# A hybrid decoder layer in float32: first products by arrival, one triangle product fewer, values' products turned round, bias rows in fp32r

## The chip, the cores and the metric

The kernel runs on one core of a Trainium2 chip. The metric is the device time of one execution in microseconds; before the change it is 813.0 us, the median of three runs (812.77 to 813.18). TensorE multiplies (PE in the profile; its weight loads are PEld), VectorE is DVE, ScalarE is ACT, GpSimd is POOL, and SyncE (SP) issues most of the loads.

## The reference

One decoder layer on 512 rows of 1024 columns. A normalized input is projected once; three token mixers read the projection: attention in a sliding window of 128 with sinks and a T5 bias by distance, stick-breaking attention, and attention to 256 rows of memory. Each mixer's output is gated, the three are summed and projected, and a SwiGLU network follows. What the change touches is the stick-breaking mixer and the bias:

```python
z = einsum('bqhd,bkhd->bhqk', q, k) * (d ** -0.5)
log_1m = where(causal, log_sigmoid(-z), 0.0)
between = lax.cumsum(log_1m, axis=3, reverse=True) - log_1m
a = where(causal, exp(log_sigmoid(z) + between), 0.0)
out = einsum('bhqk,bkhd->bqhd', a, v)
```

It has 8 heads of width 64 and 4 blocks of 128 rows. The bias of the window is `rel_bias[t5_bucket(dist)]`, one row of distances per head.

## The kernel before

**Number formats.** Most products keep float32 accuracy with three products of the type fp32r: an operand is split into a high part (a ScalarE copy, line 134) and the rest (a VectorE subtraction, line 135), and `mm3` (lines 166 to 168) adds high by high, high by low, low by high. `mm` (line 171) is one product in the type of its operands. A product of plain float32 operands shows as two instructions, called passes here.

**Streams.** Dense work (projections `kb`, `qb`, `ka`, `qa`, gates `g`, values `pv`, memory keys `pmk` and values `pmv`, branch outputs) lies in one list of units. `Stream` loads weights ahead, splits them ahead and gives the products out in small pieces. The attention code calls `dn.run(us)` between its steps, so that some microseconds of dense products stand between one step and the next in the program.

**Order.** The instructions go through the framework's scheduler, which keeps program order as priority and lets later work go ahead of work whose operands it holds to be late. The start alone is ordered by hand (lines 503 to 545). PSUM has a pool of two banks for dense work (`dps`) and one of six (`aps`) for attention.

**Start.** Eleven products on zeros (`WARM`) come first. Then the first three weight matrices (`his`, `los`), which arrive in pieces, meet the eight chunks of x (`u[k]`, high `uh`, low `ul`, lines 237 and 238). Three generators, one for each matrix, are advanced in turn; each turn is one `mm3`. So chunk 0 is multiplied as three products for matrix 0, three for matrix 1, three for matrix 2, and so on.

**Bias rows.** `band_bias` (lines 567 to 595) copies the table on GpSimd, multiplies it by a one-hot matrix in one float32 product of 384 columns over 32 rows, adds the window's mask on VectorE and stores the rows through DRAM. It follows the values' projection, whose results VectorE takes out of PSUM into `v_all` (line 333).

**A head of stick-breaking attention** (`sb_head`, lines 605 to 673). Scores lie with keys on partitions: key block j needs only the queries from block j on, so the four blocks have 512, 384, 256 and 128 columns. Blocks 0 and 1 fill the tiles `z[0]` and `z[1]`; blocks 2 and 3 share `z[2]`. ScalarE and VectorE make the softplus `e` and its parts `sh` and `sl`; of `e[2]` a further 128 columns hold the sum of blocks 2 and 3. Then the running sums over keys are added in PSUM: a triangle of -1 (`ntri_r`) within each block, a matrix of -1 (`none_r`) for the later blocks. Blocks 0 to 2 use the two fp32r parts, block 3 uses plain float32 (`ntri`, lines 660 and 661). Three exponentials (line 663, in the order of the tiles) give the weights, and 3 us of dense work follow. After the odd head of a pair, eight products with `v_all` add up the pair's output `ysb` in one bank: four key blocks for the even head on partitions 0 to 63 and four for the odd head on partitions 64 to 127, block 0 (512 columns) first, the even head ahead of the odd one (lines 670 to 672). In plain float32 these are 16 passes for each of four pairs.

Of the kernel before, what the change touches and what calls it, by code (L numbers as in the profile page):

```python
# [10 lines left out]
F32 = mybir.dt.float32  # L11
# [3 lines left out]
ALU = mybir.AluOpType  # L15
# [11 lines left out]
SWA, SB, MEM = 0, 1, 2  # L27
LOAD_AHEAD = 4
SPLIT_AHEAD = 3
WARM = 11  # L30


class Stream:
# [70 lines left out]
def tile_kernel(ctx, tc, a):  # L104
# [22 lines left out]
    def aps(name):  # L127
        return psa.tile([P, 512], F32, tag="a", name=name)
# [39 lines left out]
        nc.tensor.matmul(out, ll, rh, start=False, stop=stop, skip_group_check=True)  # L168

    def mm(out, l, r, start, stop):  # L170
        nc.tensor.matmul(out, l, r, start=start, stop=stop, skip_group_check=True)  # L171

    def cols(hl, o, n):
        return hl[0][:, o : o + n], hl[1][:, o : o + n]
# [86 lines left out]
    def stack_twice(kind, idx, t):  # L261

        for e in range(2):
# [9 lines left out]
            nc.vector.tensor_copy(x[o : o + 64, :], t[r : r + 64, :])  # L273
            st[(kind + "s", idx, e)] = x

    def proj(kind, idx):
        def gen(hi, lo):
            ps = (aps if kind == "kb" or (kind, idx) == ("qb", 2) else dps)(f"{kind}{idx}")
            for k in range(KC):
                mm3(ps[:, :], cols((hi, lo), k * P, P), u[k], k == 0, k == KC - 1)  # L280
                yield 0.65
            t = ck(f"{kind}{idx}")
            s = 0.125 if kind in ("qa", "qb") else 1.0

            def evac():
                with tc.high_priority():
                    nc.vector.scalar_tensor_tensor(t[:, :], ps[:, :], s, st["rb"][:, :], op0=ALU.mult, op1=ALU.mult)  # L287
                if kind in ("kb", "qa"):
                    stack_parts(kind, idx, t)
                elif kind in ("qb", "ka"):  # L290
                    stack_twice(kind, idx, t)
                elif kind == "qm":
                    st[("qms", idx)] = parts(f"qms{idx}", t)

            if "rb" in st:
                evac()
            else:
                st.setdefault("waiting", []).append(evac)
            st[(kind, idx)] = t

        return gen
# [43 lines left out]
    def vcols(t, lo):  # L345
        return v_all[:, t * 640 + lo : t * 640 + lo + 64]
# [156 lines left out]
    with tc.manual_schedule():  # L503

        idle = cst.tile([P, 512], BF16, name="idle")
        nc.vector.memset(idle[:, :], 0.0)
        pw = dps("warm")
        for i in range(WARM):
            mm(pw[:, :], idle[:, :P], idle[:, :], True, True)

        first_load(nc.scalar, 0)
        first_table = nc.scalar.preload_act_table_set("natural_log_exp_and_others")
        load_x(0, 3)
        first_load(nc.sync, 1)
        load_x(3, 5)
        first_load(nc.sync, 2)
        load_x(5, 8)
        dn.loaded = dn.have = FIRST
        first_split(0, 0)
        gain_split(0)  # L520
        for i in range(1, FIRST):
            first_split(i, 0)
        gain_split(1)
        gain_split(2)
        for p in (1, 2):
            for i in range(FIRST):
                first_split(i, p)
            for k in range(*PIECE[p]):
                if u[k] is None:
                    gain_split(k)  # L530
        xacc = ck("xacc")
        nc.scalar.activation(xacc[:, :], xraw[0][:, :], AF.Square)
        for k in range(1, KC):
            nc.scalar.activation(xraw[k][:, :], xraw[k][:, :], AF.Square)
            nc.vector.tensor_tensor(xacc[:, :], xacc[:, :], xraw[k][:, :], op=ALU.add)
        dn.ahead(4, 3)
        gens = [dn.units[i]["mm"](his[i], los[i]) for i in range(FIRST)]
        for k in range(KC + 1):
            for g in gens:
                next(g, None)  # L540
        dn.at = FIRST
        st["rs"], st["rb"] = rstd_of("x", xacc, S, aps)
        st["chain"] = since[-1]
        for f in st.pop("waiting"):
            f()
# [21 lines left out]
    def band_bias():  # L567
        oh = ck("oh")
        nc.sync.dma_start(oh[:32, :384], a["onehot"])
        rbt = ck("rbt")  # L570
        nc.sync.dma_start(rbt[:32, :8], a["rel_bias"])
        wm = ck("wm")
        nc.sync.dma_start(wm[:, :384], a["winmask"])

        rb16 = ck("rb16")
        nc.gpsimd.tensor_copy(
            rb16[:32, :P].rearrange("b (h j) -> b h j", h=8), rbt[:32, :8].unsqueeze(2).to_broadcast([32, 8, 16])
        )
        ps = aps("pbias")
        mm(ps[:, :384], rb16[:32, :P], oh[:32, :384], True, True)  # L580
        row = ck("brow")
        nc.vector.tensor_tensor(row[:, :384], ps[:, :384], wm[:, :384], op=ALU.add)
        scr = drm.tile([8, P * 384], F32, name="bscr")
        nc.gpsimd.dma_start(
            scr[:, :].rearrange("h (j m i) -> (h j) m i", j=16, m=8),
            row[:, :384].unsqueeze(1).to_broadcast([P, 8, 384]),
        )
        out = []
        for i in range(4):
            b = ck(f"bias{i}")  # L590
            src = scr[2 * i : 2 * i + 2, 127:383]
            src = bass.AP(src.tensor, src.offset, [[383, P], [P * 384, 2], [1, 256]])
            nc.gpsimd.dma_start(b[:, :].rearrange("p (h k) -> p h k", h=2), src)
            out.append(b)
        return out
# [9 lines left out]
    def sb_head(h):  # L605
        c = h // 2
        ks, qs, ql = (st[(x, c, h % 2)] for x in ("kbs", "qbs", "qbl"))
        z = [aps(f"z{h}{i}") for i in range(3)]

        def seg(ts, j):  # L610
            i, o, n = SEG[j]
            return ts[i][:, o : o + n]

        for j in range(4):
            i, o, n = SEG[j]
            kj = slice(j * P, (j + 1) * P)
            if j < 3:
                out, qh, qlo = z[i][:, o : o + n], qs[:, j * P :], ql[:, j * P :]
            else:

                out = z[i][:, o : o + 2 * n]
                qh = qs[:, j * P :].unsqueeze(1).to_broadcast([P, 2, P])
                qlo = ql[:, j * P :].unsqueeze(1).to_broadcast([P, 2, P])
            mm(out, ks[:, kj], qh, j < 3, False)
            mm(out, ks[:, kj], qlo, False, False)

        for i in range(2):
            mm(z[i][:, :P], identb[:, :], negm[:, :], False, False)
        blocks23 = z[2][:, :].rearrange("p (b n) -> p b n", b=4)[:, 0:4:2, :]
        mm(blocks23, identb[:, :], negm[:, :].unsqueeze(1).to_broadcast([P, 2, P]), False, False)  # L630
        e = [ck(f"e{h}{i}") for i in range(3)]
        sh = [ck(f"sh{h}{i}", F32R) for i in range(3)]
        sl = [ck(f"sl{h}{i}", F32R) for i in range(3)]
        for i in range(3):
            x, n = e[i][:, : W[i]], W[i]
            nc.scalar.activation(x, z[i][:, :n], AF.Abs)
            fn(x, x, AF.Exp, scale=-1.0)
            st["chain"] = fn(x, x, AF.Ln, bias=1.0)
            nc.vector.scalar_tensor_tensor(x, z[i][:, :n], 0.0, x, op0=ALU.max, op1=ALU.add)  # L639
            if i == 2:  # L640

                nc.vector.tensor_tensor(e[i][:, 384:], e[i][:, 128:256], e[i][:, 256:384], op=ALU.add)
                x, n = e[i][:, :], 512
            nc.vector.tensor_copy(sh[i][:, :n], x)
            nc.vector.tensor_tensor(sl[i][:, :n], x, sh[i][:, :n].bitcast(F32), op=ALU.subtract)
        yield 7.0

        def both(t):

            return t[2][:, :].rearrange("p (b n) -> p b n", b=4)[:, 0:4:3, :]  # L650

        for j in range(3):
            for t in (sh, sl):
                mm(seg(z, j), ntri_r[:, :], seg(t, j), False, j == 2 and t is sl)
        for t in (sh, sl):
            mm(z[0][:, 128:], none_r[:, :], seg(t, 1), False, False)
        for t in (sh, sl):
            mm(z[0][:, 256:], none_r[:, :], both(t), False, t is sl)
            mm(z[1][:, 128:384], none_r[:, :], both(t), False, t is sl)
        mm(z[2][:, 128:256], none[:, :], seg(e, 3), False, True)  # L660
        mm(seg(z, 3), ntri[:, :], seg(e, 3), False, True)
        for i in range(3):
            fn(e[i][:, : W[i]], z[i][:, : W[i]], AF.Exp)
        yield 3.0
        if h % 2 == 0:
            st["even"] = e
            return

        ys = aps(f"ysb{c}")
        for j in range(4):  # L670
            for i, x in enumerate((st["even"], e)):
                mm(ys[64 * i : 64 * i + 64, j * P :], vcols(j, 128 + (2 * c + i) * 64), seg(x, j), j == 0, j == 3)
        pair_out(SB, c, ys)


# [728 lines left out]
```

## Time and profile before

| | us |
|---|---|
| median of three runs | 813.0 |
| the profiled execution | 813.07 |
| its span | 811.3 |
| PE busy in it | 802.9 |
| DVE busy | 588.7 |
| ACT busy | 439.6 |

The 1.8 us between the profiled execution's time and its span lie outside the program's instructions. In the timeline a row gives the start, the length, the engine, the line and the operation; equal instructions that follow one another are one row with their count, under the shape of the first. The length of a product goes on into the next one's, so the cost of a product in a dense row of them is the distance between two starts. In brackets stand the idle time of the engine before the row and what ended it.

### The profile page before, as it was taken

The numbers are of one execution on the slowest core, as the hardware profiler recorded it, in microseconds if no ns is written. First come the engines' busy times: TensorE is split into PE (matmuls) and PEld (weight loads), VectorE is DVE, ScalarE is ACT, GpSimd is POOL, SyncE is SP. The second block draws the span as 40 slices with busy tenths as digits, with TensorE's granted clock in tenths as the row PEclk, the third lists the DMA queues.
The fourth block names the chain that finished last, engine by engine and source line by source line (L and its number), as shares of the span: only waits on it lengthen the run. The fifth ranks groups of instructions, "written<-read, shape, count | busy, mean of one in ns | idle before, by whom it ended". The sixth has DMA issues, their size and how long they took to land.

```text
span 811.3 us, 12342 instructions
## 1 busy us (share of the span) xinstructions
PE 802.9 (99%) x4727; PEld 704.0 (87%) x4727; DVE 588.7 (73%) x937; ACT 439.6 (54%) x787; POOL 87.5 (11%) x105
## 2 busy tenths in 40 slices
PE   9999999999999999999999999999999999999996
PEld 6899887878788888888888899999999999988885
DVE  7895867647488843773384869877676767898797
ACT  7562766555555543552362567555455555666573
POOL 1202200000000000231004200010000000205200
PEclk9999999999999999999999999999999999999998
DMA  7434525211221223212359946877767652759902
GB/s 269 142 123 139 182 79 159 76 52 53 78 78 53 79 78 104 78 53 85 97 159 376 242 80 155 248 209 201 195 176 191 170 174 89 173 133 221 214 1 104
DMA packets 37692, 112.95 MB, mean 139 GB/s; under 512 B 4480, under 2 KB 6192, under 8 KB 37632
## 3 DMA queue, kind: packets, MB, share of 16 engines
q1 hardware_dynamic: 29184, 86.32, 32.5%
q0 software_dynamic: 8016, 25.44, 16.3%
q8 instruction: 37, 0.61, 0.3%
q10 hardware_dynamic: 432, 0.39, 0.1%
q14 instruction: 23, 0.19, 0.1%
HBM read 108.46 MB, written 3.67 MB: 138 GB/s over the span
## 4 chain that ended last, share of the span: by engine, by line
PE 98%; DMA 0%; ACT 0%; DVE 0%; issue 0%; DVEq 0%
PE g L166 5%; PE g L167 5%; PE g L168 5%; PE gx L166 5%; PE gx L168 5%; PE gx L167 5%; PE z L171 4%; PE br L167 3%; PE br L166 3%; PE br L168 3%; PE gy L168 3%; PE gy L166 3%; PE gy L167 3%; PE x L168 2%; PE x L167 2%; PE x L166 2%
## 5 line engine op out<-in xcount | busy, mean ns | idle before, releaser
L134 ACT CAST hi<-gw 128x1024 fp32r<-128x1024 f32 x77 | 79.7, 1047 | 83.1 <-DVE gw L989 39.9
L134 ACT CAST hi<-raw 128x1024 fp32r<-128x1024 f32 (+2 forms) x64 | 65.8, 1034 | 103.7 <-issue 57.2
L135 DVE TENSOR_TENSOR lo<-gw,hi 128x1024 fp32r<-128x1024 f32 x77 | 93.4, 1224 | 32.4 <-ACT hi L134 32.4
L135 DVE TENSOR_TENSOR lo<-raw,hi 128x1024 fp32r<-128x1024 f32 (+2 forms) x64 | 78.2, 1222 | 16.9 <-ACT hi L134 16.6
L166 PE MATMUL g<-uh,hi 128*128 128x512 f32 x192 | 75.6, 394 | 0.0
L167 PE MATMUL g<-ul,hi 128*128 128x512 f32 x192 | 74.8, 390 | 0.0
L168 PE MATMUL g<-uh,lo 128*128 128x512 f32 x192 | 74.8, 390 | 0.0
L287 DVE SCALAR_TENSOR_TENSOR g<-g,rb_x 128x512 f32<-128x512 f32 x24 | 16.4, 690 | 55.3 <-PE g L168 55.2
L971 POOL DMA_DIRECT2D gw<-in_w_gu x27 | 23.4, 905 | 187.9 <-DMA gw<-in_w_gu 115.3
L168 PEld LDWEIGHTS g<-uh,lo 128*128 128x128 f32 x192 | 36.1, 188 | 7.6
L166 PEld LDWEIGHTS g<-uh,hi 128*128 128x128 f32 x192 | 36.1, 188 | 7.5 <-issue 0.3
L167 PEld LDWEIGHTS g<-ul,hi 128*128 128x128 f32 x192 | 36.1, 188 | 7.1
L134 ACT CAST hi<-r 128x1024 fp32r<-128x1024 f32 (+1 forms) x24 | 23.5, 981 | 19.9 <-PE y L168 5.3
L167 PE MATMUL x<-lo,lh 128*128 128x512 f32 x88 | 34.3, 390 | 0.0
L166 PE MATMUL x<-hi,lh 128*128 128x512 f32 x88 | 34.3, 389 | 0.0
L168 PE MATMUL x<-hi,ll 128*128 128x512 f32 x88 | 34.1, 389 | 0.0
L135 DVE TENSOR_TENSOR lo<-r,hi 128x1024 fp32r<-128x1024 f32 (+1 forms) x24 | 27.2, 1133 | 3.7 <-ACT hi L134 3.6
L184 ACT ACTIVATE e<-e 128x384 f32<-128x384 f32 (+1 forms) x48 | 26.9, 561 | 1.5
L134 ACT CAST hi<-bp 128x512 fp32r<-128x512 f32 x33 | 19.1, 619 | 13.4 <-PE y L168 4.8
L135 DVE TENSOR_TENSOR lo<-bp,hi 128x512 fp32r<-128x512 f32 x33 | 22.4, 714 | 4.8 <-ACT hi L134 4.7
L166 PE MATMUL gx<-B11h,hi 128*128 128x256 f32 x88 | 25.1, 286 | 0.2 <-ACT B11h L900 0.2
L639 DVE SCALAR_TENSOR_TENSOR e<-z,e 128x384 f32<-128x384 f32 (+1 forms) x24 | 14.3, 598 | 15.0 <-ACT e L184 15.0
(539 smaller groups left out, 2627.2 us busy)
## 6 DMA issues: line engine op xcount, KB each, us to landing
gw<-in_w_gu SPq DMA_DIRECT2D x57, 512.0 KB, 4.8
raw<-in_w_p SPq DMA_DIRECT2D x38, 512.0 KB, 3.3
gw<-in_w_gu POOLq DMA_DIRECT2D x27, 512.0 KB, 7.1
raw<-in_w_br SPq DMA_DIRECT2D x12, 512.0 KB, 3.7
bp<-in_w_dn SPq DMA_DIRECT2D x22, 256.0 KB, 8.1
r<-in_w_dn POOLq DMA_DIRECT2D x10, 512.0 KB, 8.3
raw<-in_w_out SPq DMA_DIRECT2D x8, 512.0 KB, 3.6
bp<-in_w_dn POOLq DMA_DIRECT2D x11, 256.0 KB, 12.8
```

The costliest lines, as they stand in the source:

```text
L134: ins = nc.scalar.copy(hi, raw)
L135: lows = nc.vector.tensor_tensor(lo, raw, hi.bitcast(F32), op=ALU.subtract)
L166: nc.tensor.matmul(out, lh, rh, start=start, stop=False, skip_group_check=True)
L167: nc.tensor.matmul(out, lh, rl, start=False, stop=False, skip_group_check=True)
L168: nc.tensor.matmul(out, ll, rh, start=False, stop=stop, skip_group_check=True)
L171: nc.tensor.matmul(out, l, r, start=start, stop=stop, skip_group_check=True)
L184: ins = nc.scalar.activation(*args, **kw)
L287: nc.vector.scalar_tensor_tensor(t[:, :], ps[:, :], s, st["rb"][:, :], op0=ALU.mult, op1=ALU.mult)
L639: nc.vector.scalar_tensor_tensor(x, z[i][:, :n], 0.0, x, op0=ALU.max, op1=ALU.add)
L971: nc.gpsimd.dma_start(gw[(n, key)][:, :], g_src(n, i, j), accum_op=ALU.add)
```

## The change

Four edits, and one warm-up product fewer.

1. The products of chunk 0 with the first three weight matrices are written out in an order of their own; the generators go on from chunk 1.
2. The bias table is split on GpSimd into two fp32r parts, the one-hot matrix is copied to fp32r, and two fp32r products take the place of the float32 one.
3. The triangle product of key block 2 covers all 384 columns of `z[2]`, block 3 included, in the two fp32r parts; the float32 triangle product of block 3 is gone.
4. The values' products run from block 3 to block 0, the odd head ahead of the even one.

```diff
-WARM = 11
+WARM = 10
...
+    first_ps = {}
     def proj(kind, idx):
         def gen(hi, lo):
-            ps = (aps if kind == "kb" or (kind, idx) == ("qb", 2) else dps)(f"{kind}{idx}")
-            for k in range(KC):
+            begun = first_ps.get((kind, idx))
+            ps = begun or (aps if kind == "kb" or (kind, idx) == ("qb", 2) else dps)(f"{kind}{idx}")
+            for k in range(1 if begun else 0, KC):
...
+        for i in range(FIRST):
+            first_ps[("kb", i)] = aps(f"kb{i}")
+        for n, (i, w, r) in enumerate(
+            ((0, his, 0), (0, los, 0), (1, his, 0), (0, his, 1), (1, his, 1), (1, los, 0), (2, his, 0), (2, his, 1), (2, los, 0))
+        ):
+            mm(first_ps[("kb", i)][:, :], w[i][:, :P], u[0][r], n in (0, 2, 6), False)
         gens = [dn.units[i]["mm"](his[i], los[i]) for i in range(FIRST)]
-        for k in range(KC + 1):
+        for k in range(1, KC + 1):
...
+        ohr, rbh, rbl = ck("ohr", F32R), ck("rbh", F32R), ck("rbl", F32R)
+        nc.gpsimd.tensor_copy(ohr[:32, :384], oh[:32, :384])
+        nc.gpsimd.tensor_copy(rbh[:32, :P], rb16[:32, :P])
+        nc.gpsimd.tensor_tensor(rbl[:32, :P], rb16[:32, :P], rbh[:32, :P].bitcast(F32), op=ALU.subtract)
         ps = aps("pbias")
-        mm(ps[:, :384], rb16[:32, :P], oh[:32, :384], True, True)
+        for x in (rbh, rbl):
+            mm(ps[:, :384], x[:32, :P], ohr[:32, :384], x is rbh, x is rbl)
...
         for j in range(3):
             for t in (sh, sl):
-                mm(seg(z, j), ntri_r[:, :], seg(t, j), False, j == 2 and t is sl)
+                mm(z[j][:, : W[j]], ntri_r[:, :], t[j][:, : W[j]], False, j == 2 and t is sl)
...
         mm(z[2][:, 128:256], none[:, :], seg(e, 3), False, True)
-        mm(seg(z, 3), ntri[:, :], seg(e, 3), False, True)
...
-        for j in range(4):
-            for i, x in enumerate((st["even"], e)):
-                mm(ys[64 * i : 64 * i + 64, j * P :], vcols(j, 128 + (2 * c + i) * 64), seg(x, j), j == 0, j == 3)
+        for j in (3, 2, 1, 0):
+            for i, x in ((1, e), (0, st["even"])):
+                mm(ys[64 * i : 64 * i + 64, j * P :], vcols(j, 128 + (2 * c + i) * 64), seg(x, j), j == 3, j == 0)
```

More of the change, by code (lines that the diff above doesn't have):

```diff
@@ L170, in mm @@
     def mm(out, l, r, start, stop):
-        nc.tensor.matmul(out, l, r, start=start, stop=stop, skip_group_check=True)
+        return nc.tensor.matmul(out, l, r, start=start, stop=stop, skip_group_check=True)
     def cols(hl, o, n):
```

## The prediction

> **What bounds the kernel now.** I read the page first, then who waits for whom, then the timeline of the three places that the change touches.
>
> ```profile
> span 811.3 us, 12342 instructions
> ...
> PE 802.9 (99%) x4727; PEld 704.0 (87%) x4727; DVE 588.7 (73%) x937; ACT 439.6 (54%) x787; POOL 87.5 (11%) x105
> ...
> PE 98%; DMA 0%; ACT 0%; DVE 0%; issue 0%; DVEq 0%
> ```
>
> The span is 811.3 us and 98% of the chain that ended last is matmul. The waits of PE itself are almost nothing; besides 1.3 us before the first warm-up product, the longest is this one, in the start that the change rewrites:
>
> ```profile
> PE kb L167 <- DVE ul L238: 0.3, 1, 0.3
> ```
>
> So this kernel is a queue of products on TensorE. An edit gains what it takes out of that queue, unless the products behind then arrive ahead of their operands. For each part I ask both.
>
> **Start (order of the first nine products, one warm-up product less).**
>
> ```profile
> 1.35 4.26 PE L171 MATMUL warm<-idle 128*128 128x512 bf16 x11 [1.35 <-DVE idle L506]
> ...
> 5.45 0.50 PE L166 MATMUL kb<-uh,hi_first 128*128 128x512 f32 x1
> ...
> 6.24 0.50 PE L167 MATMUL kb<-ul,hi_first 128*128 128x512 f32 x1 [0.29 <-DVE ul L238]
> ...
> 6.92 0.42 DVE L135 TENSOR_TENSOR lo_first<-raw_first,hi_first 128x256 fp32r<-128x256 f32 x1 [0.40 <-ACT hi_first L134]
> ...
> 7.55 1.41 DVE L238 SCALAR_TENSOR_TENSOR ul<-xT,xg,uh 128x512 fp32r<-128x512 f32 x2 [0.20 <-ACT uh L237]
> ...
> 8.35 0.19 PEld L167 LDWEIGHTS kb<-ul,hi_first 128*128 128x128 f32 x1 [0.21 <-DVE ul L238]
> 8.41 0.44 PE L167 MATMUL kb<-ul,hi_first 128*128 128x512 f32 x1
> ```
>
> The second real product waits from 5.45 to 6.24 for the low part of the first chunk of x. The new order fills that hole with products whose parts are there, so the nine first products can end about 0.5 us sooner; the last part they need, the third matrix's low part, is there at 6.92 + 0.42 = 7.34. But the second product of the next chunk needs the second `ul`, whose weight load starts at 8.35 because VectorE gives the two `ul` one after the other from 7.55. No order on TensorE changes VectorE's queue. That product starts at 8.41 now and can start at 8.35 then: 0.06 us, and a hole of some 0.5 us opens just before it. What is late next is therefore `ul` of chunk 1. The warm-up row ends at 1.35 + 4.26 = 5.61, modelled drain included, and the first real product starts at 5.45 already: the eleventh warm-up product is hidden now and its removal gives nothing. Bounds: 0 to 0.1 us; I take 0.06.
>
> **Bias rows.** One fp32 product runs as two passes; the new one is two fp32r products of the same 384 columns.
>
> ```profile
> 66.44 1.29 POOL L576 COPY rb<-rbt 32x128 f32<-32x128 f32 x1
> ...
> 77.72 1.92 DVE L333 TENSOR_SCALAR v_all<-pv,rs_x 128x320 f32<-128x320 f32 x4
> ...
> 78.91 0.91 PE L171 MATMUL pbias<-oh,rb 32*128 32x384 f32 x2
> ...
> 79.75 0.19 PEld L171 LDWEIGHTS z<-qbs,kbs 128*128 128x128 f32 x1 [0.55 <-DVE v_all L333]
> ```
>
> The two passes hold TensorE from 78.91 to 79.75, 0.84 us. By the 128-column price of the next part (two fp32 passes of 128 columns 0.21) two of 384 are 0.64, so 0.20 are the edges, where the tile changes to 32 rows and back. An fp32r product of 384 columns takes 0.18 from its start to the next one's (102.75 to 102.93, below). Two of them with the same edges are 0.56, a gain of 0.28; I take 0.3. The weight load behind has a named wait on VectorE's `v_all`, whose four run until 77.72 + 1.92 = 79.64; if that wait is real, `z` still starts near 79.7 and the gain is 0.05. I take the larger: that pool has six PSUM banks, `v_all` reads four of them, and the bias product and the first `z` can have the other two. Range 0.05 to 0.4. The three new GpSimd instructions cost nothing on the path: `rb` is made by 67.73, the 1.29 us copy of 128 columns prices them at 3 + 1 + 1 such copies, 6.5 us, done near 74.2, and TensorE wants them at 78.9. Behind them on GpSimd stands only the issue of the bias rows' store, which waits for the product anyway.
>
> **Triangle product.** The first pair of heads:
>
> ```profile
> 102.75 0.34 PE L171 MATMUL z<-sl,ntri_r 128*128 128x384 f32 x1
> 102.93 0.28 PE L171 MATMUL z<-sh,ntri_r 128*128 128x256 f32 x1
> 103.04 0.34 PE L171 MATMUL z<-sh,none_r 128*128 128x384 f32 x1
> ...
> 103.18 1.23 DVE L135 TENSOR_TENSOR lo<-raw,hi 128x1024 fp32r<-128x1024 f32 x1 [0.53 <-ACT hi L134]
> ...
> 103.72 1.07 PE L171 MATMUL ysb<-e,v_all 128*64 128x512 f32 x2
> ...
> 104.72 0.39 PE L166 MATMUL pmk<-mh,hi 128*128 128x256 f32 x1
> ...
> 105.06 0.28 PE L168 MATMUL pmk<-mh,lo 128*128 128x256 f32 x1
> ...
> 106.96 0.38 PE L171 MATMUL z<-e,none 128*128 128x128 f32 x2
> 107.04 1.36 ACT L184 ACTIVATE e<-z 128x512 f32<-128x512 f32 x3 [0.74 <-PE z L171]
> 107.17 0.39 PE L171 MATMUL z<-e,c_ntri 128*128 128x128 f32 x2
> 107.32 0.36 PE L166 MATMUL pmk<-mh,hi 128*128 128x256 f32 x1
> ...
> 110.51 0.28 PE L168 MATMUL pmk<-mh,lo 128*128 128x256 f32 x1
> 110.72 2.37 PE L171 MATMUL ysb<-e,v_all 128*64 128x512 f32 x14
> 113.02 0.50 PE L171 MATMUL z<-qbs,kbs 128*128 128x512 f32 x1
> ```
>
> Durations overlap, so I price by starts. 256 columns of fp32r take 0.11 us (102.93 to 103.04), 384 take 0.18. Two products widen, at +0.06 each. The fp32 product of 128 columns, two passes, goes: its twin `none` takes 0.21 (106.96 to 107.17), so 0.22. Per head 0.22 - 0.12, about 0.11 with the unrounded starts; eight heads, 0.9 us. The wide `sh` and `sl` hold block 3's columns already (line 643 widens the split to 512), so no wait is added. Range 0.5 to 0.9.
>
> **Values' products.** Here lies most. Each of the 8 products of a pair is two passes; the even head writes rows 0 to 63, the odd head rows 64 to 127. The first, the even head's, is ready long before the odd head's, and the scheduler uses it as a filler: alone from 103.72 to 104.72, 1.00 us, plus 0.10 to enter (110.51 to 110.72 is 0.21 for a product that takes 0.11) and 0.12 behind it (104.72 to 105.06 is 0.34 for two). That is 1.22 us with half the array idle. The other 14 passes take 2.30 us (110.72 to 113.02). By the 128-column price, 0.21 for two passes, the four widths of one head come to 0.21 + 0.43 + 0.64 + 0.86 = 2.14 us. So 2.30 is one head's time: the other head's run beside it. In the new order the odd head's product of block 3 comes first, and that waits for the last of three exponentials; nothing can be drawn ahead, and all 16 passes should take the same 2.3 us. All four pairs have such a lone product:
>
> ```profile
> 125.24 1.07 PE L171 MATMUL ysb<-e,v_all 128*64 128x512 f32 x2
> 125.29 1.22 DVE L135 TENSOR_TENSOR lo<-raw,hi 128x1024 fp32r<-128x1024 f32 x1
> ...
> 127.04 0.40 PE L167 MATMUL pmv<-lo,mh 128*128 128x512 f32 x1
> ...
> 171.24 1.07 PE L171 MATMUL ysb<-e,v_all 128*64 128x512 f32 x2
> 171.74 1.22 DVE L135 TENSOR_TENSOR lo<-raw,hi 128x1024 fp32r<-128x1024 f32 x1
> ...
> 173.61 0.39 PE L168 MATMUL g<-uh,lo 128*128 128x512 f32 x1
> ...
> 204.50 1.07 PE L171 MATMUL ysb<-e,v_all 128*64 128x512 f32 x2
> ```
>
> What did the filler hide? In pair 1 the first product that reads the low part of the next weights is at 105.06; that part is there at 103.18 + 1.23 = 104.41, so only 0.60 of 1.22 is real (0.05 for the signal). Pair 2: 125.29 + 1.22 = 126.51 against 127.04, 0.48. Pair 3: 172.96 against 173.61, 0.61. In pair 4 what follows has its operands, 1.22. The triangle's 0.11 stands in the same holes in pairs 2 and 3, so 2.7 us are left in all, if nothing else fills. If the scheduler finds another filler (the next head's `z`, for which a bank of PSUM is free longer now), up to 4 x 1.22 = 4.9. I take 3.2, near the low end, since it is what the rows show.
>
> Sum: 0.06 + 0.3 + 0.9 + 3.2 = 4.46 us. The profiled execution took 813.07 us, 1.8 over its span, and the median is 813.0; 813.07 - 4.46 = 808.6. The forecast's own range goes from all high ends (0.1 + 0.4 + 0.9 + 4.9 = 6.3, 806.8; and 0.6 more for an order that I can't see, 806.2) to low ends with 2.0 of the values' part (0.05 + 0.5 + 2.0; 810.5). About 0.2%, 1.6 us, is what can be told from no change.
>
> **A rule against it.**
>
> ```profile
> 110.70:110.80 0.10, 0.08 (x2) 0.08 (x4) 0.00 (x0) 0.00 (x0) 1.00 0.00 0
> ```
>
> Restricted to `ysb`, two passes start within this 0.1 us, though a 512-column pass lasts 0.43: they are of two products, so the narrower product did not wait for the wider one's second pass. The Trainium skill, "TensorE: Matmul & The Clock Gate", Part 3, states that matmuls start and end strictly in program order. The trace disagrees, if the two passes of a product stand together in the queue.
>
> **The rivals.** (1) Strict order between the halves. Then in a block of rising widths each second half starts one pass late, and at the end the widest pass stands alone: 0.43 per pair, 1.7 us, 810.3. The 0.1 us row speaks against it. 6%. (2) The wait takes the place of the filler: the block is put right behind the triangle products, and TensorE stands until the last exponential, from 107.40 (107.17 + 0.22) to 108.40 (107.04 + 1.36), 1.0 us in four pairs. Everything on TensorE is queued behind it. The sum shrinks to 0.5: 812.6. Against it: three microseconds of other products lie between now, and stand ahead in the program. 8%. (3) The lone product stays, some other one being drawn ahead: 1.3 us left, 811.8. 3%. (4) Slower: the halves come apart. If the even head's four products may run ahead of the odd head's, being ready, each half runs alone: 2.14 + 0.36 for its edges, twice, 5.0 us, against 1.22 + 2.53 now, +1.25 in four pairs, with 1.3 gained elsewhere: 816.8. It decides as soon as the two widest products (1.5 us) run apart in each pair. For it: they are ready. Against: they are ready now too, and only the first was drawn ahead; the others stood behind the odd head's. 5%.
>
> **The numbers.** The forecast has 78%. Faster: forecast and (1), and a little of (2), 0.85; within 0.2%: the rest of (2), (3), 0.10; slower: (4), 0.05. The range 806.2 to 811.2 takes the forecast's own and (1) and leaves out 16%.
>
> **What would show it.** Right: `ysb` in four groups of 16 passes at 2.3 to 2.5 us and none of 2; no `c_ntri`, `z<-sh,ntri_r` with 16 of 384 columns; the bias product under 0.6 us; a new wait of 0.4 to 0.5 us on `ul` near 8.35; new PE waits on `lo` of about 0.6 us near 104, 126 and 172. Wrong: groups of 8 or fewer passes, waits of PE on the exponentials ahead of `ysb`, or a `z` that still starts 0.05 us after `v_all`.

## The result, and the profile after

The changed kernel takes 808.64 us, the median of six runs (808.40 to 808.81), against 813.07 before (six runs); the ratio is 0.9946, with an interval of 0.9933 to 0.9958. It is 4.43 us faster; 4.46 were forecast. The profiled execution took 808.77 us. Its page:

```profile
span 807.0 us, 12317 instructions
...
PE 797.5 (99%) x4710; PEld 701.1 (87%) x4710; DVE 587.3 (73%) x937; ACT 439.7 (54%) x787; POOL 88.7 (11%) x108
...
PE 96%; DVE 1%; ACT 1%; DMA 1%; issue 1%; ACTq 0%; DVEq 0%
```

TensorE has 17 instructions fewer: one warm-up product and eight float32 triangle products of two passes. The bias product keeps its count, as two products of one pass. VectorE and ScalarE have as many instructions as before. The waits of TensorE, all of them:

```profile
PE warm L171 <- DVE idle L509: 1.3, 1, 1.3
PE ysb L171 <- ACT e L184: 1.1, 1, 1.1
PE kb L167 <- DVE ul L238: 0.2, 1, 0.2
PE pmv L166 <- DVE mk L383: 0.2, 1, 0.2
PE gx L166 <- ACT B11h L916: 0.2, 1, 0.2
```

Two rows are new: one wait on the exponentials ahead of `ysb`, and 0.2 us on a memory key. No wait on the low parts `lo` is there. The timeline of the first pair, where the lone product of 1.00 us and the 14 passes stood:

```profile
108.98 0.28 PE L168 MATMUL pmk<-mh,lo 128*128 128x256 f32 x1
109.19 2.37 PE L171 MATMUL ysb<-e,v_all 128*64 128x128 f32 x16
111.50 0.50 PE L171 MATMUL z<-qbs,kbs 128*128 128x512 f32 x1
```

All 16 passes take 2.31 us (109.19 to 111.50), as long as the 14 did. Pairs 3 and 4 look the same. Pair 2 does not:

```profile
136.63 0.38 PE L171 MATMUL z<-e,none 128*128 128x128 f32 x2
136.71 1.36 ACT L184 ACTIVATE e<-z 128x512 f32<-128x512 f32 x3 [0.81 <-PE z L171]
...
138.12 0.44 PE L171 MATMUL ysb<-e,v_all 128*64 128x128 f32 x4 [1.11 <-ACT e L184]
138.49 0.50 PE L166 MATMUL qa<-uh,hi 128*128 128x512 f32 x1
...
142.48 0.39 PE L168 MATMUL qa<-uh,lo 128*128 128x512 f32 x1
142.80 2.15 PE L171 MATMUL ysb<-e,v_all 128*64 128x256 f32 x12
144.88 0.50 PE L171 MATMUL z<-qbs,kbs 128*128 128x512 f32 x1
```

There the first products of `ysb` stand right behind the triangle products. They need the last of the three exponentials, which ends at 136.71 + 1.36 = 138.07, and TensorE stands until 138.12. Only four passes follow, and the other twelve come 4 us later. Why the scheduler cuts the block in two here and in no other pair is not shown.

The start and the bias rows:

```profile
7.67 1.41 DVE L238 SCALAR_TENSOR_TENSOR ul<-xT,xg,uh 128x512 fp32r<-128x512 f32 x2 [0.20 <-ACT uh L237]
...
7.87 0.39 PE L166 MATMUL kb<-uh,hi_first 128*128 128x512 f32 x1
...
8.48 0.50 PE L167 MATMUL kb<-ul,hi_first 128*128 128x512 f32 x1 [0.22 <-DVE ul L238]
...
78.82 0.31 PE L168 MATMUL pv<-hi,ul 128*128 128x320 f32 x1
79.06 0.44 PE L171 MATMUL pbias<-ohr,rbh 32*128 32x384 f32 x1
79.34 0.33 PE L171 MATMUL pbias<-ohr,rbl 32*128 32x384 f32 x1
79.61 0.50 PE L171 MATMUL z<-qbs,kbs 128*128 128x512 f32 x1
```

The predicted hole before the second `ul` is there: such products stand 0.23 us apart where nothing is waited for, but here the next one starts 0.61 us after 7.87. (The row names `ul` for 0.22 of it; 0.4 to 0.5 had been forecast.) The stretch from the last `pv` product (78.82) to the first `z` (79.61) is 0.79 us; before it was 1.08 (78.67 to 79.75): 0.29 us.

**Where the time went.** The stretch from the first `z` product to the first transposition after the mixers (`ut`) holds both edits of stick-breaking attention and no start. It ran from 79.75 to 462.74 before and from 79.61 to 458.44 after:

```profile
458.44 0.38 PE L928 MATMUL ut<-c_ident,mt 128*128 128x128 f32 x2
```

That is 382.99 and 378.83 us, 4.16 less. With 0.29 of the bias rows and a start that took 0.15 longer in this execution, the span's 4.3 are accounted for.

### The profile page after: what moved, and what is told of

Read it like the earlier page. It is cut to its first block, busy times and chain, and to the rows that moved or that the text cites. A ratio compares the mean times of both kernels' runs of the same rounds, so it can differ in the third digit from the quotient of the medians.

```text
span 807.0 us, 12317 instructions
## 1 busy us (share of the span) xinstructions
PE 797.5 (99%) x4710; PEld 701.1 (87%) x4710; DVE 587.3 (73%) x937; ACT 439.7 (54%) x787; POOL 88.7 (11%) x108
## 4 chain that ended last, share of the span: by engine, by line
PE 96%; DVE 1%; ACT 1%; DMA 1%; issue 1%; ACTq 0%; DVEq 0%
PE g L166 5%; PE g L168 5%; PE g L167 5%; PE gx L166 5%; PE gx L168 5%; PE gx L167 5%; PE z L171 3%; PE br L166 3%; PE br L167 3%; PE br L168 3%; PE gy L168 3%; PE gy L166 3%; PE gy L167 3%; PE x L166 2%; PE x L168 2%; PE x L167 2%
```

## The experiments

Two theories of the prediction are tested. The first: time is gained by the lone product of each pair, which the order of the heads removes. The second: where that filler is gone, a wait opens, on the low parts of weights (the prediction's sum) or on the exponentials (its second rival). The stretch from the first `z` to `ut` of each run is given beside its time, since it leaves out the start, whose length differs from execution to execution (below). A stretch is read from one profiled execution, a time is a median. Each ratio is taken against the runs of the kernel before that were made beside that kernel; their medians lie between 813.07 and 813.21.

| kernel | us | ratio and interval | stretch, against before |
|---|---|---|---|
| the change | 808.64 | 0.9946 [0.9933, 0.9958] | -4.16 |
| values_alone | 809.45 | 0.9952 [0.9940, 0.9965] | -3.62 |
| values_heads_only | 808.43 | 0.9940 [0.9927, 0.9952] | -4.44 |
| values_blocks_only | 811.55 | 0.9978 [0.9969, 0.9987] | -1.58 |
| triangle_alone | 812.78 | 0.9994 [0.9985, 1.0003] | -0.49 |
| bias_alone | 812.99 | 1.0000 [0.9991, 1.0008] | +0.05 |
| all_old_start | 808.59 | 0.9945 [0.9933, 0.9958] | -4.16 |
| all_warm11 | 808.74 | 0.9950 [0.9937, 0.9962] | -4.19 |
| all_block0_first | 808.45 | 0.9943 [0.9929, 0.9957] | -4.91 |
| all_exp_last_first | 808.64 | 0.9942 [0.9928, 0.9955] | -4.52 |
| old_start_block0_first | 807.94 | 0.9935 [0.9922, 0.9947] | -4.91 |

**The values' products alone.**

```diff
-        for j in range(4):
-            for i, x in enumerate((st["even"], e)):
-                mm(ys[64 * i : 64 * i + 64, j * P :], vcols(j, 128 + (2 * c + i) * 64), seg(x, j), j == 0, j == 3)
+        for j in (3, 2, 1, 0):
+            for i, x in ((1, e), (0, st["even"])):
+                mm(ys[64 * i : 64 * i + 64, j * P :], vcols(j, 128 + (2 * c + i) * 64), seg(x, j), j == 3, j == 0)
```

> Only the values' products turned round, nothing else of the change. Theory (the lone product): the early product of the even head is gone in all four pairs, 1.22 us each, and one wait on the exponentials of about 1.2 us opens in pair 2, as in the changed kernel: about 3.4 us faster, 809.7; ysb in three groups of 16 passes and one in two pieces. Rival (the low parts of weights are late once the filler is gone, as predicted): 2.7 us, 810.4, with PE waits on lo. Rival (the gain of the whole change lies in the triangle product): under 1 us.

The stretch is 3.62 us shorter, with three groups of 16 passes and one group in two pieces. Besides the wait before the first warm-up product and one of 0.2 us in the network behind the mixers, which all these kernels have, TensorE waits for this:

```profile
PE ysb L171 <- ACT e L184: 0.9, 1, 0.9
PE kb L167 <- DVE ul L238: 0.3, 1, 0.3
```

No wait on `lo`: the theory that the prediction's sum rested on falls, and the other one holds. By pairs, from the starts of the heads' first triangle products (for pair 4, to the product behind the block), 1.17 us are gained at pair 1, 0.09 at pair 2, 1.19 at pair 3 and 1.17 at pair 4. A pair gives almost the whole lone product or, where the wait stands, almost nothing.

**Which half of the reorder does it.** First the heads alone, then the blocks alone.

```diff
         for j in range(4):
-            for i, x in enumerate((st["even"], e)):
+            for i, x in ((1, e), (0, st["even"])):
```

> Only the order of the two heads turned (odd head first), the key blocks still from 0 to 3. Theory (the lone product): which head comes first decides, so no product runs ahead; the first product needs only the first exponential, so the wait in pair 2 falls from 1.2 us to about 0.4: 4.2 us faster, 808.9. Rival (the direction of the blocks decides): no gain, 813.0.

The stretch is 4.44 us shorter, 0.8 more than with both. Pair 2 now:

```profile
136.61 1.36 ACT L184 ACTIVATE e<-z 128x512 f32<-128x512 f32 x3 [0.69 <-PE z L171]
136.75 0.39 PE L171 MATMUL z<-e,c_ntri 128*128 128x128 f32 x2
...
137.26 1.72 PE L171 MATMUL ysb<-e,v_all 128*64 128x512 f32 x8
```

Block 0 needs the first exponential only, so `ysb` starts 0.65 us after the exponentials begin instead of 1.41 (136.71 to 138.12).

```diff
-        for j in range(4):
+        for j in (3, 2, 1, 0):
             for i, x in enumerate((st["even"], e)):
-                mm(ys[64 * i : 64 * i + 64, j * P :], vcols(j, 128 + (2 * c + i) * 64), seg(x, j), j == 0, j == 3)
+                mm(ys[64 * i : 64 * i + 64, j * P :], vcols(j, 128 + (2 * c + i) * 64), seg(x, j), j == 3, j == 0)
```

> Only the order of the key blocks turned (3 to 0), the even head still first. Theory (the lone product): the even head's product of 128 columns is drawn ahead in place of the one of 512, alone for 0.21 + 0.36 us instead of 1.22, so 0.6 us per pair less the wait of about 1.2 us in pair 2: 1.2 to 2.4 us faster, 810.7 to 811.9. Rival (the direction of the blocks decides): as values_alone, 809.7.

```profile
103.88 0.43 PE L171 MATMUL ysb<-e,v_all 128*64 128x128 f32 x2
104.25 0.39 PE L171 MATMUL z<-sl,ntri_r 128*128 128x256 f32 x1
```

With the even head first a product still runs ahead alone; it is only shorter, 0.37 us here in place of 1.00. In pair 2 the lone product waited 0.9 us on the exponentials. The gain is 1.58 us, within what was expected. So the order of the heads removes the lone product. With the odd head first, turning the blocks costs 0.8 us; with the even head first it makes the lone product shorter.

**The triangle product alone.**

```diff
-                mm(seg(z, j), ntri_r[:, :], seg(t, j), False, j == 2 and t is sl)
+                mm(z[j][:, : W[j]], ntri_r[:, :], t[j][:, : W[j]], False, j == 2 and t is sl)
...
-        mm(seg(z, 3), ntri[:, :], seg(e, 3), False, True)
```

> Only the triangle product of block 3 in the two fp32r parts. Theory: 0.11 us in each of eight heads, 0.9 us, 812.2. Rival (it stands in holes that other waits hold open): 0.5 us or less, 812.6 or more.

The stretch is 0.49 us shorter, half of what was expected and as much as the rival gave; the time is 0.34 shorter, which its interval doesn't tell from nothing. The even head of pair 2 shows where the rest is. First the kernel before, then this one:

```profile
124.51 0.38 PE L171 MATMUL z<-e,none 128*128 128x128 f32 x2
124.73 0.39 PE L171 MATMUL z<-e,c_ntri 128*128 128x128 f32 x2
```

```profile
124.92 0.38 PE L171 MATMUL z<-e,none 128*128 128x128 f32 x2
125.65 1.07 PE L171 MATMUL ysb<-e,v_all 128*64 128x512 f32 x2 [0.35 <-ACT e L184]
```

Before, the two triangle passes stood between `none` and `ysb`, which came 0.73 us after `none` (124.51 to 125.24); it comes 0.73 after it here. The passes left, and a wait on the exponential took their place. The two wider products cost their 0.12 all the same. In the odd head of pair 2 the block of `ysb` starts 0.65 us after the exponentials begin in both kernels (139.85 to 140.50 before, 140.20 to 140.85 here). So from head to head the stretch changes by -0.12 and -0.11, then by +0.10 over the two heads of pair 2, then by -0.07 to -0.11 in each of the last four. The same holds beside the other edits: between values_alone and the change the stretch shrinks by 0.54, by heads -0.12 and -0.11, then +0.05 over the two heads of pair 2, then -0.07 to -0.11 each. There it is the wait on the memory key, on VectorE, that is new in the even head (0.2 us), and the wait on the exponentials in the odd head grows from 0.9 to 1.1.

**The bias rows alone.** The diff is that of the change, with nothing else.

> Only the bias rows in two fp32r products. Theory (the passes held TensorE): 0.3 us faster, 812.8, z starts 0.3 us earlier. Rival (z waits for v_all): 0.05 us or nothing, 813.0.

The time does not tell (ratio 1.0000), the trace does: from the last `pv` to the first `z` 0.79 us, where all kernels with the float32 product have 1.08. `z` follows 0.29 us sooner, as the theory says. The last of the four `v_all` ends at 79.73 here, and `z` starts at 79.55: `z` did not wait for it.

**The start.** The whole change with the old order and eleven warm-up products, and the whole change with eleven alone.

```diff
-WARM = 10
+WARM = 11
...
-        for k in range(1, KC + 1):
+        for k in range(KC + 1):
```

(The first run leaves out the nine products written by hand as well.)

> The whole change but with the first products in the old order and eleven warm-up products. Theory (the second ul bounds the start whatever the order): as the changed kernel within 0.1 us, 808.6, and the second product of chunk 1 again some 0.06 us after its ul. Rival (the new order gains): 0.3 to 0.5 us slower than the changed kernel, 809.0.

> The whole change with eleven warm-up products instead of ten. Theory: no difference, 808.6, since the first real product waits for uh. Rival (the eleventh stands in the way, or its lack delays the granted clock): 0.2 to 0.4 us either way.

808.59 and 808.74 stand beside 808.64. By the time, neither the order nor the warm-up product can be told from nothing. The first product that follows the three matrices (`ss_x`) starts at 22.56 before, but anywhere from 22.23 to 23.07 in the eight profiles with the old order, and from 22.48 to 23.50 in the five with the new one. That scatter is larger than any gain of this edit.

The traces tell more when `ss_x` is measured from the start of the second `ul`. In all five profiles with the new order it comes 14.99 to 15.04 us later, in six of the eight with the old order as well, 15.11 and 15.31 in the other two. So the second `ul` sets the end of the start, and the order of the products hardly moves it. What scatters is that `ul` itself, from 7.24 to 8.47. It stands behind a ScalarE cast of the third matrix, which waits for its load. The latest one, in all_block0_first:

```profile
7.40 0.40 ACT L134 CAST hi_first<-raw_first 128x256 fp32r<-128x256 f32 x1 [1.93 <-DMA raw_first<-in_w_p]
...
8.47 1.41 DVE L238 SCALAR_TENSOR_TENSOR ul<-xT,xg,uh 128x512 fp32r<-128x512 f32 x2 [0.20 <-ACT uh L237]
```

In the kernel before the same cast waits 0.71 us, and the `ul` starts at 7.55. The eleventh warm-up product is not always hidden: in four of the nine profiles that have it the first real product starts at 5.66 only, 0.4 us or more after VectorE could begin the first `ul`, which needs the same `uh`. The two starts of 15.11 and 15.31 are among these four.

**The wait in pair 2.** Three ways to shorten it: block 0 first, the third exponential first, and block 0 first with the old start.

```diff
-        for j in (3, 2, 1, 0):
+        for j in range(4):
             for i, x in ((1, e), (0, st["even"])):
-                mm(ys[64 * i : 64 * i + 64, j * P :], vcols(j, 128 + (2 * c + i) * 64), seg(x, j), j == 3, j == 0)
+                mm(ys[64 * i : 64 * i + 64, j * P :], vcols(j, 128 + (2 * c + i) * 64), seg(x, j), j == 0, j == 3)
```

> The whole change, but the values' products from block 0 to block 3 with the odd head first. Theory (the wait in pair 2 is the distance from the first to the last exponential, 0.86 us): that wait falls from 1.1 us to about 0.3, the rest stays: 0.8 us faster than the changed kernel, 807.8. Rival (the new order makes the scheduler place the products otherwise): no gain or slower, 808.6 or more.

```diff
-        for i in range(3):
+        for i in (2, 1, 0):
             fn(e[i][:, : W[i]], z[i][:, : W[i]], AF.Exp)
```

> The whole change, with the three exponentials of a head in the order 2, 1, 0, so that the one that the first product of a pair needs runs first. Theory (in pair 2 TensorE stands 1.2 us until the third exponential ends): the first products come after one exponential, some 0.6 us sooner, and those of block 0 still wait for nothing, since they come last: 0.6 us faster than the changed kernel, 808.0. Rival (what stands there is not the exponentials but the scheduler's place for the block): no difference, 808.6.

> Bias rows, triangle product and the odd head first as in the change, but key blocks from 0 to 3 and the old start with eleven warm-up products. Theory: 0.75 us faster than the changed kernel by the stretch from the first head to the last pair, which all_block0_first's trace has, and nothing for the start: 807.9. Rival (the median of 808.45 of all_block0_first says that something else takes it back): 808.5.

With block 0 first the stretch is 0.75 us shorter than in the change, and the wait of TensorE ahead of `ysb` in pair 2 falls from 1.11 to 0.35. This is the row of the last kernel:

```profile
137.49 1.08 PE L171 MATMUL ysb<-e,v_all 128*64 128x512 f32 x4 [0.35 <-ACT e L184]
```

With the exponentials turned in the program, the scheduler still runs the 512-column one first, and the needed one can come second; the wait falls to 0.73:

```profile
136.94 1.36 ACT L184 ACTIVATE e<-z 128x512 f32<-128x512 f32 x3 [0.81 <-PE z L171]
...
137.97 0.87 PE L171 MATMUL ysb<-e,v_all 128*64 128x128 f32 x8 [0.73 <-ACT e L184]
```

The stretch follows, 0.36 us shorter than in the change. So the wait is on the exponentials, and its price is the distance to the one that the first product needs: 0.38 and 0.76 us less wait made the stretch 0.36 and 0.75 us shorter. old_start_block0_first is the fastest kernel measured, 807.94 us; its interval overlaps that of the change. all_block0_first has the same stretch and 808.45. Its profiled execution, of 808.80 us, lost the difference in the start, where the second `ul` came at 8.47 as shown above, behind a load and not behind a product. Its other four executions have no trace, so that the new order has no part in the medians' 0.5 us is likely but not shown.

**Why no low part was late.** The whole change with weights split one unit ahead instead of three.

```diff
-SPLIT_AHEAD = 3
+SPLIT_AHEAD = 1
```

> The whole change with weights split one unit ahead of their use instead of three. It tells why no wait on the low parts opened where the prediction had put three. Theory (a low part made at that moment is for a unit up to three places later): with one place of lead, PE waits on lo of 0.3 to 1 us appear in the stick-breaking stretch, and the time rises by several us. Rival (the low parts are never late here): no waits on lo and no change beyond 0.5 us.

With this edit the kernel no longer computes the layer. The edit reaches the feed-forward network too, where weights are added up in place and split; that a split there takes a sum at the wrong time is likely, but not shown. Only waits of the mixers are read, not the 826.25 us, which is a single run. Two of them are on low parts:

```profile
PE pmv L167 <- DVE lo L135: 0.5, 1, 0.5
...
PE pmk L168 <- DVE lo L135: 0.4, 1, 0.4
```

With three units of lead there was none. The built program of before, which names the buffers, says the same: the part that VectorE makes at 103.18 is `lo_1120`, and the `pmk` product at 105.06 reads `lo_922`. These are the first readers of the two parts, with their places among TensorE's instructions:

```
536 L168 MATMUL pmk_1124<-mh_792,lo_922 128x256
...
634 L168 MATMUL pmk_1297<-mh_792,lo_1120 128x256
```

Between the two lie 98 instructions and two other parts, `lo_983` and `lo_1081`.

## Why the prediction was right, and which steps were not

The total was right, 808.6 against 808.64, and so was the gain in the largest term, the lone product. Two steps were wrong: one gave 0.4 us too much, the other 0.4 too little. That they cancelled to 0.03 us is luck. Two of the prediction's own signs of being wrong appeared, a group of fewer than eight passes and a wait on the exponentials ahead of `ysb`, both in pair 2; its new waits on `lo` did not.

**Bias rows: right.** 0.3 forecast, 0.29 in the traces of the change and of bias_alone. The count of banks decided it rightly against the named wait. The three new GpSimd instructions took 1.3 us (67.74 to 69.01 in after), not the estimated 6.5; nothing hung on it.

**Start: the mechanism right, the size not testable.** The hole before the second `ul` opened as described (0.6 us between two products), and that `ul` sets the end of the start whatever the order. 0.06 us can't be seen under a scatter of 0.8. That the eleventh warm-up product is hidden was read from one profile; in four of nine it was not, and the start then ended 0 to 0.3 us later behind the second `ul` than elsewhere.

**Triangle product: mis-sized.** 0.9 forecast, 0.5 measured. The price per head was about right, 0.07 to 0.12 in six heads. The step that failed is "so no wait is added": in the two heads of pair 2 the shorter row of products stands ahead of steps whose start ScalarE and VectorE set, and they took it back. The forecast's low end, 0.5, was the value.

**Values' products: near in sum, wrong in what is lost.** 3.2 forecast, 3.62 alone. The lone product's price was right, 1.22 forecast, 1.17 to 1.19 gained in each of pairs 1, 3 and 4. The failed step is "only 0.60 of 1.22 is real" and its two neighbours. It took the low part that VectorE was making beside the product that reads a low part a microsecond later as the same one, by the name of the tile alone. They are three units apart, so nothing waited, and the 2.2 us that the rows were read to lose (4.9 less 2.7) did not come. In their place came the second rival in one pair of four: 1.1 us on the last exponential. The rival's own counter-argument, that 3 us of dense products lie between, was read from pair 1 (107.32 to 110.51) and carried over to all; in pair 2 already the kernel before starts the block 0.5 us after it starts the last triangle product (139.99 to 140.50), with one product of scores between.

**Strict order between the halves: refuted here.** Counts, durations in ns, first and last start of the products of `ysb` that run between 111.42 and 111.43 and between 111.61 and 111.64 in the first pair of before, then of those at the end of the first pair of after:

```profile
L171 PE MATMUL ysb<-e,v_all x3: 379/486/592, 111.1 to 111.4; 128*64 128x384 f32 x1, 128*64 128x512 f32 x1, 128*64 128x256 f32 x1
```

```profile
L171 PE MATMUL ysb<-e,v_all x3: 379/487/592, 111.2 to 111.6; 128*64 128x512 f32 x1, 128*64 128x256 f32 x1, 128*64 128x384 f32 x1
```

```profile
L171 PE MATMUL ysb<-e,v_all x2: 592/592/592, 111.0 to 111.0; 128*64 128x512 f32 x2
```

In before the program has all products of 384 columns ahead of those of 256. Yet a pass of 256 columns starts at 111.43, ahead of two of the four passes of 384 columns, the first of which starts at 111.63: the narrower product of one head did not wait for the wider one of the other. In after two passes of 512 columns start together, though one lasts 0.43 us: they are of the two heads. The 16 passes take 2.31 us with rising widths, where a second half one pass late would have given 2.7. By the Trainium skill, "TensorE: Matmul & The Clock Gate", Part 3, starts and ends keep program order; the traces of this kernel differ from that in the starts of products on different halves of the columns.

## What to carry to other kernels

Products that use half the array pay only in company: put first the one whose operand comes last, so that a scheduler can't spend a half-array product as a filler, and among those choose the block whose operand comes first. Before a wait is charged to a removed filler, find the buffer number, not the tile's name, and check each place of a repeated pattern, since one of four behaved otherwise. A saving that stands ahead of a wait set by another engine was worth nothing there.

## What the runs showed of the hardware

Two things had not been expected. Products on the two column halves of the array run side by side, passes of both heads starting within 0.1 us of each other, and a pass of one half starting 0.2 us ahead of an earlier one of the other half (the rows above); 16 passes take 2.31 us, where the widths of one head alone add up to an estimated 2.14. And one and the same start, in the profiles of eight kernels, ends anywhere within 0.8 us with the arrival of its first loads, so that an edit of the start below half a microsecond needs its own stretch or many runs.
